# A two-layer decoder trunk on one core: the token factor of the input RMSNorm is applied to the projections' results instead of to their operand

## The chip, the cores and the metric

One Trainium2 chip, one of its cores. The kernel is a single program on that core; its time is the device time of one execution in microseconds (us). The median of three executions before the change is 2590.63 us (2590.49 to 2591.32).

## The reference, cut to what matters

Two identical layers run over 256 tokens with 2048 channels, in float32. Of one layer, what the change touches is this:

```python
h = rmsnorm(x, pre_norm)            # x * rsqrt(mean(x*x) + eps) * pre_norm
proj = h @ w_in                     # 2048 x 21728 combined input projection
(m_z, m_xbc, m_dt, f_q, f_k, f_v, f_f, f_gate, g_q, g_k, g_v, g_lr, g_gate,
 l_cq, l_ckv, l_kr, l_gate, merge) = jnp.split(proj, ...)
xbc = jax.nn.silu(causal_depthwise_conv(m_xbc, conv_w, conv_b))   # a convolution over tokens
...                                  # four branches: SSD, forgetting attention, GLA, latent attention
gates = jax.nn.sigmoid(merge.reshape(bsz, s, N_BRANCHES, D_MODEL))
mixed = sum(gates[:, :, b] * (out[b] @ w_branch[b]) for b in range(4))
return x + rmsnorm(mixed @ w_out, post_norm)
```

The norm has two factors: one per channel (`pre_norm`) and one per token (the reciprocal root of that token's mean square). A factor per token commutes with the projection: `(r * x * pre) @ w = r * ((x * pre) @ w)`.

## The kernel before, in words

All large products are made in float32 precision out of three float32r matmuls: each operand is split into a rounded part and a remainder (`hh` and `hl` for the normed and transposed x, `hi` and `lo` for a weight tile), and hi·hh, lo·hh and hi·hl are accumulated. Weights come as 512 KB tiles `raw` of 128x1024, through the SyncE DMA queue into five buffers; `fetch` (L154) lets ScalarE copy a tile to `hi` (L158) and VectorE subtract to get `lo` (L159). `hi` and `lo` have three buffers each, so the split runs up to two tiles ahead of TensorE.

`chunk_a` (L165) makes 512 output columns for both 128-token blocks (tt = 0 and 1) in one two-bank accumulator `acc`: 16 slices k of the 2048 channels, by two token blocks, by three matmuls of 128x512 are 96 matmuls. Its result has tokens on the partitions. `chunk_b` (L186) makes the transposed result, 4 blocks of 128 output channels on the partitions by 256 tokens, with 192 matmuls of 128x256. There are two `acc` buffers, so a result has to be read out before the next chunk but one begins. The very first chunk of a layer (`acc_c`, L368) takes its first three weight tiles as one group: k = 0 to 5 for token block 0, then k = 0 to 5 for block 1, and from k = 6 on both blocks in turn.

The input norm is `norm_x` (L307). For one token block it sums the squares of x on ScalarE (L238), gets the factor r by a power on GpSimd (L62), multiplies x by r on VectorE (L316 in the first layer; L318 in the second, where the row `prow` with the channel factor is multiplied in as well), transposes the product on TensorE in four tiles of four 128x128 blocks (L321, `tr_x`, two PSUM buffers), and splits the transposed tile into `hh` on ScalarE (L325, L330) and `hl` on VectorE (L327, L331). In the first layer the channel factor comes in there, as a per-partition scalar `vec`. The second layer's x is the end of the first: with the last output projection `acc_y` in hand, L862 adds the post-normed rows to the residual `xr`, in four pieces of 512 columns for each token block, and `norm_x` starts from there.

The order within each engine is set by a scheduler that places the program's instructions by a simulated timeline; work of a background generator (`bg`, `step`, `drain`) is written between the weight tiles of a chunk. Each engine then runs its own list strictly in order and waits on semaphores. The attention, GLA and SSD cores run in such generators beside the projections.

Of the kernel before, what the change touches and what calls it, by code (L numbers as in the profile page):

```python
# [37 lines left out]
def trunk(ctx: ExitStack, tc: tile.TileContext, x, pos, vecs, rows, dskip, pre, post, glaw2,  # L38
# [33 lines left out]
    nc.scalar.dma_start(ident, consts[:, C_ID:C_ID + P])  # L72
    vec = cp.tile([P, DEPTH, V_N], F32, tag="vec", name="vec")
    nc.scalar.dma_start(vec, vecs.rearrange("l p v -> p l v"))
# [16 lines left out]
    def mask_tables():  # L91
        cst = sl.tile([P, 2048], F32, tag="s7", name="cst")
        nc.sync.dma_start(cst[:, :C_N], consts)
        nc.sync.dma_start(caus, consts[:, C_CAUS:C_CAUS + P])
        nc.sync.dma_start(negm, consts[:, C_NEGM:C_NEGM + P])
        S.copy(id2, cst[:, C_ID2:C_ID2 + 32])
        V.tensor_copy(lvl, cst[:, C_LVL:C_LVL + 1024].rearrange("p (a b) -> p a b", a=8))
        yield
# [55 lines left out]
    def fetch(src, n=1024, own=None):  # L154
        raw = st.tile([P, 1024], F32, tag="raw", name="raw", bufs=5)
        nc.sync.dma_start(raw[:, :n], src)
        hi, lo = own or (st.tile([P, 1024], F32R, tag=t, name=t, bufs=3) for t in ("hi", "lo"))
        S.copy(hi[:, :n], raw[:, :n])  # L158
        V.tensor_tensor(lo[:, :n], raw[:, :n], hi[:, :n].bitcast(F32), ALU.subtract)  # L159
        return hi, lo  # L160
# [146 lines left out]
    def norm_x(tt, src, dst, ssq, prow):  # L307

        tot = small([P, 1], f"xtot{tt}")
        V.tensor_reduce(tot, ssq, AX.X, ALU.add)  # L310
        r = rstd(tot, D, 1, f"xn{tt}")
        ts_ = slice(tt * P, (tt + 1) * P)
        for c in range(4):
            cs = slice(c * 512, (c + 1) * 512)
            if prow is None:
                V.tensor_scalar(dst[:, cs], src[:, cs], r, None, ALU.mult)  # L316
            else:
                V.scalar_tensor_tensor(dst[:, cs], src[:, cs], r, prow[:, cs], ALU.mult, ALU.mult)  # L318
            pt = psT(f"tr_x{tt}{c}").rearrange("p (b t) -> p b t", b=4)
            for j in range(4):  # L320
                PE.transpose(pt[:, j], dst[:, c * 512 + j * P:c * 512 + (j + 1) * P], ident)  # L321
            if prow is None:
                pw = lambda j: vec[:, 0, V_PRE + 4 * c + j:V_PRE + 4 * c + j + 1]
                for j in range(4):
                    S.activation(hh[:, 4 * c + j, ts_], pt[:, j], AF.Copy, scale=pw(j))  # L325
                for j in range(4):
                    V.scalar_tensor_tensor(hl[:, 4 * c + j, ts_], pt[:, j], pw(j),  # L327
                                           hh[:, 4 * c + j, ts_].bitcast(F32), ALU.mult, ALU.subtract)
            else:
                S.copy(hh[:, 4 * c:4 * c + 4, ts_], pt)  # L330
                V.tensor_tensor(hl[:, 4 * c:4 * c + 4, ts_], pt, hh[:, 4 * c:4 * c + 4, ts_].bitcast(F32),  # L331
                                ALU.subtract)
# [7 lines left out]
    ssq0 = small([P, 2, 2], "xssq")  # L340
    junk0 = slot(6, "junk")
    for tt in range(2):
        for c in range(2):
            cs = slice(c * 1024, (c + 1) * 1024)
            sumsq(xt[tt][:, cs], junk0[:, cs], ssq0[:, tt, c:c + 1])
        norm_x(tt, xt[tt], slot(2 + tt, "xn"), ssq0[:, tt], None)

    for l in range(DEPTH):
# [15 lines left out]
        for i in range(2):  # L364
            if l == 0 and i == 1:
                bg.append(mask_tables())
                bg.append(rope_tables())
            acc = chunk_a(w_in[l], nxt(8), 16, hh, hl, 0, "acc_c", [3, 1, 1, 1, 1, 1] if i == 0 else None)  # L368
            S.copy(cc[:, i], acc)
            for tt in range(2):  # L370
                sumsq(acc[:, tt], ropej[:, 0:2].rearrange("p a t -> p (a t)"), cssq[:, 2 * i + tt:2 * i + tt + 1])
# [12 lines left out]
        raw2 = slot(6, "raw2")  # L384
        krope, krr = raw2[:, 1024:1024 + T], raw2[:, 1280:1280 + T]
# [130 lines left out]
        for i in range(2):  # L516
            acc = chunk_b(w_in[l], nxt(8), 4, hh, hl, "acc_g")
            if i == 0:
                S.activation(gqk[:, i], acc, AF.Copy, scale=128 ** -0.5)
            else:  # L520
                V.tensor_copy(gqk[:, i], acc)
# [147 lines left out]
        for c in range(3):  # L669
            acc = chunk_b(w_in[l], nxt(8), 4, hh, hl, "acc_x")  # L670
            dst = xsT[:, 4 * c:4 * c + 4] if c < 2 else bcT[:, 0:4]
            for j in range(4):
                b = 4 * c + j
                cw = lambda i: vc(V_CW + 4 * b + i)
                S.activation(dst[:, j], acc[:, j], AF.Identity, bias=vc(V_CB + b), scale=cw(3))
                for i in range(1, 4):
                    V.scalar_tensor_tensor(dst[:, j, i:], acc[:, j, :T - i], cw(3 - i), dst[:, j, i:],
                                           ALU.mult, ALU.add)
# [152 lines left out]
        if not last:  # L831
            prow = load_row(4, pre, l + 1, "prow")
# [7 lines left out]
        ssq = small([P, 2, 4], "xssq4")  # L840
        for c in range(4):
# [9 lines left out]
            for tt in range(2):  # L851
# [8 lines left out]
                for q in range(4):  # L860
                    qs = slice(q * 512, (q + 1) * 512)
                    V.scalar_tensor_tensor(xr[tt][:, qs], yt[tt][:, qs], r, xr[tt][:, qs], ALU.mult, ALU.add)  # L862
                    if not last:
                        sumsq(xr[tt][:, qs], yt[tt][:, qs], ssq[:, tt, q:q + 1])
# [5 lines left out]
                if not last:  # L870
                    norm_x(tt, xr[tt], yt[tt], ssq[:, tt], prow)
# [21 lines left out]
def _layout(inp):  # L893
# [37 lines left out]
    for lv in range(7):  # L931
# [8 lines left out]
            "dskip": inp["d_skip"], "pre": inp["pre_norm"], "post": inp["post_norm"], "glaw2": inp["gla_w2"], "w_sm": w_sm, "w_in": w_in,  # L940
# [20 lines left out]
```

## Time and profile before

| what | value |
|---|---|
| median of 3 executions | 2590.63 us |
| the profiled execution: its own time / the span of its instructions | 2591.68 us / 2589.3 us |
| VectorE busy in the span | 1531.6 us (59%) |
| ScalarE busy in the span | 1248.9 us (48%) |
| DMA moved / mean rate | 461.48 MB / 178 GB/s |
| mean granted TensorE clock | 0.997 |

A row of the timeline view gives the start in us from the span's start, the duration in us, the engine, the source line, the operation with output and inputs, how many equal instructions were merged, and in brackets how long the engine had been idle and what released it. ACT is ScalarE, DVE is VectorE, POOL is GpSimd, SPq and ACTq are the DMA-issuing queues of SyncE and ScalarE. Matmul durations overlap, so the distance between two starts is what a matmul costs TensorE. In the waits view a row reads "engine, tile, line, released by": total us, times, longest.

### The profile page before, as it was taken

What the parts mean: (1) busy time and instruction counts of PE and PEld (TensorE: products, weight loads), DVE (VectorE), ACT (ScalarE), POOL (GpSimd) and SP (SyncE); (2) the same over time, 40 slices, a digit from 0 to 9 for tenths busy, and PEclk for the clock granted to TensorE, in tenths of its full rate; (3) what the DMA queues carried; (4) which work ended last, traced back from release to release, by engine and by line L of the source; (5) the groups of instructions that cost most, each with busy time, mean ns of one, the idle gap of its engine ahead of it and who ended that gap; (6) DMA issues with size and microseconds to landing.
All of it is one profiled execution on the core that took longest, in us unless ns stands there. A gap on an engine that the chain in (4) does not pass through costs nothing.

```text
span 2589.3 us, 34775 instructions
## 1 busy us (share of the span) xinstructions
PE 2558.0 (99%) x13810; PEld 2208.8 (85%) x13810; DVE 1531.6 (59%) x1886; ACT 1248.9 (48%) x1589; POOL 25.1 (1%) x33
## 2 busy tenths in 40 slices
PE   8999999999999999999989999999999999999998
PEld 6898888988899888888878988889888998888887
DVE  6755855676654455555557568546766545555554
ACT  5654544455444445444455445444555444544443
POOL 0000000000000000000000000000000000000000
PEclk9999999999999999999999999999999999999999
DMA  6554555555555555655645445555555555556554
GB/s 228 181 161 147 170 164 186 183 178 170 179 195 180 173 177 173 209 189 182 211 158 186 155 147 175 168 180 185 174 173 189 185 177 176 169 166 206 191 179 155
DMA packets 126722, 461.48 MB, mean 178 GB/s; under 512 B 14656, under 2 KB 15168, under 8 KB 125664
## 3 DMA queue, kind: packets, MB, share of 16 engines
q1 hardware_dynamic: 126144, 459.11, 54.7%
q8 instruction: 108, 1.77, 0.3%
q14 instruction: 54, 0.44, 0.0%
q10 hardware_dynamic: 416, 0.17, 0.0%
HBM read 455.02 MB, written 4.19 MB: 177 GB/s over the span
## 4 chain that ended last, share of the span: by engine, by line
PE 98%; ACT 1%; DVE 1%; issue 0%; DMA 0%; POOL 0%; SPq 0%; DVEq 0%; POOLq 0%; ACTq 0%
PE acc_f L196 2%; PE acc_f L195 2%; PE acc_f L194 2%; PE acc_mC L180 2%; PE acc_mD L180 2%; PE acc_mA L180 2%; PE acc_mC L179 2%; PE acc_mA L179 2%; PE acc_mD L179 2%; PE acc_mA L181 2%; PE acc_mC L181 2%; PE acc_mD L181 2%; PE acc_mB L181 2%; PE acc_mB L180 2%; PE acc_mB L179 2%; PE acc_y L181 2%
## 5 line engine op out<-in xcount | busy, mean ns | idle before, releaser
L159 DVE TENSOR_TENSOR lo<-raw,hi 128x1024 fp32r<-128x1024 f32 x842 | 1027.4, 1222 | 851.0 <-ACT hi L158 848.0
L158 ACT CAST hi<-raw 128x1024 fp32r<-128x1024 f32 x842 | 882.0, 1049 | 1106.8 <-PE acc_f L195 109.8
L196 PE MATMUL acc_f<-hh,lo 128*128 128x256 f32 x512 | 145.1, 283 | 0.0
L195 PE MATMUL acc_f<-hl,hi 128*128 128x256 f32 x512 | 145.0, 283 | 0.0
L194 PE MATMUL acc_f<-hh,hi 128*128 128x256 f32 x512 | 144.9, 283 | 0.0
L196 PE MATMUL acc_x<-hh,lo 128*128 128x256 f32 x384 | 108.9, 284 | 0.0
L195 PE MATMUL acc_x<-hl,hi 128*128 128x256 f32 x384 | 108.7, 283 | 0.0
L194 PE MATMUL acc_x<-hh,hi 128*128 128x256 f32 x384 | 108.7, 283 | 0.0
L180 PE MATMUL acc_mC<-lo,hh 128*128 128x512 f32 x256 | 104.6, 409 | 0.0
L180 PE MATMUL acc_mD<-lo,hh 128*128 128x512 f32 x256 | 103.1, 403 | 0.0
L180 PE MATMUL acc_mA<-lo,hh 128*128 128x512 f32 x256 | 102.7, 401 | 0.0
L179 PE MATMUL acc_mA<-hi,hh 128*128 128x512 f32 x256 | 101.9, 398 | 0.0
L179 PE MATMUL acc_mC<-hi,hh 128*128 128x512 f32 x256 | 100.5, 393 | 0.0
L180 PE MATMUL acc_mB<-lo,hh 128*128 128x512 f32 x256 | 100.2, 392 | 0.0
L181 PE MATMUL acc_mA<-hi,hl 128*128 128x512 f32 x256 | 100.1, 391 | 0.0
L179 PE MATMUL acc_mD<-hi,hh 128*128 128x512 f32 x256 | 100.0, 391 | 0.0
L181 PE MATMUL acc_mD<-hi,hl 128*128 128x512 f32 x256 | 99.8, 390 | 0.0
L181 PE MATMUL acc_mC<-hi,hl 128*128 128x512 f32 x256 | 99.8, 390 | 0.0
L181 PE MATMUL acc_mB<-hi,hl 128*128 128x512 f32 x256 | 99.7, 389 | 0.0
L179 PE MATMUL acc_mB<-hi,hh 128*128 128x512 f32 x256 | 99.7, 389 | 0.0
L194 PEld LDWEIGHTS acc_f<-hh,hi 128*128 128x128 f32 x512 | 98.3, 192 | 0.1
L195 PEld LDWEIGHTS acc_f<-hl,hi 128*128 128x128 f32 x512 | 98.3, 192 | 0.1
(419 smaller groups left out, 6040.6 us busy)
## 6 DMA issues: line engine op xcount, KB each, us to landing
raw<-in_w_in_dram SPq DMA_DIRECT2D x624, 512.0 KB, 3.4
raw<-in_w_br_dram SPq DMA_DIRECT2D x128, 512.0 KB, 3.4
raw<-in_w_out_dram SPq DMA_DIRECT2D x64, 512.0 KB, 3.4
raw<-in_w_ukv_dram SPq DMA_DIRECT2D x16, 512.0 KB, 4.3
raw<-in_w_uq_dram SPq DMA_DIRECT2D x12, 512.0 KB, 3.3
x<-in_x_dram SPq DMA_DIRECT2D x4, 512.0 KB, 5.8
xr<-in_x_dram SPq DMA_DIRECT2D x2, 1024.0 KB, 6.1
pn<-in_post_dram SPq DMA_DIRECT2D x2, 1024.0 KB, 7.0
```

The lines of the kernel that those rows point to most:

```text
L158: S.copy(hi[:, :n], raw[:, :n])
L159: V.tensor_tensor(lo[:, :n], raw[:, :n], hi[:, :n].bitcast(F32), ALU.subtract)
L179: PE.matmul(a2[tt], xh[:, k0 + k, ts_], hi[:, c], start=(k == 0), stop=False)
L180: PE.matmul(a2[tt], xh[:, k0 + k, ts_], lo[:, c], start=False, stop=False)
L181: PE.matmul(a2[tt], xl[:, k0 + k, ts_], hi[:, c], start=False, stop=(k == nk - 1))
L194: PE.matmul(acc[:, b], hi[:, c], xh[:, k], start=(k == 0), stop=False)
L195: PE.matmul(acc[:, b], hi[:, c], xl[:, k], start=False, stop=False)
L196: PE.matmul(acc[:, b], lo[:, c], xh[:, k], start=False, stop=(k == 15))
```

## The change

x goes to the transposes as it is, and the transposed tile is multiplied by the channel factor while it is split, in both layers now (`feed`). The token factor is worked out beside that (`factor`, a background generator), with one power for both token blocks, and is kept in two forms: `rt`, tokens on the partitions, and `rb`, tokens along the free axis and the same on all partitions, which two small matmuls with the identity make. Every reading of a projection's result multiplies by one of the two: per-partition scale on ScalarE (`scale_out`, the sigmoids), `scalar_tensor_tensor` with `rt` on VectorE, or a product with `rb` for the transposed results. In the first layer the DMAs are issued in another order as well: `vec` before `ident` on ScalarE's queue; on SyncE's queue the first three weight tiles between and behind the pieces of x, and the small tables `rc`, `row`, `dsk` behind the tile `cst`.

```diff
+    vec = cp.tile([P, DEPTH, V_N], F32, tag="vec", name="vec")
+    nc.scalar.dma_start(vec, vecs.rearrange("l p v -> p l v"))
+    ident = cp.tile([P, P], F32, tag="ident", name="ident")
+    nc.scalar.dma_start(ident, consts[:, C_ID:C_ID + P])
+    first_raw = []
     for tt in range(2):
         for c in range(2):
             cs = slice(c * 1024, (c + 1) * 1024)
             nc.sync.dma_start(xt[tt][:, cs], x[tt * P:(tt + 1) * P, cs])
-    ident = cp.tile([P, P], F32, tag="ident", name="ident")
-    nc.scalar.dma_start(ident, consts[:, C_ID:C_ID + P])
-    vec = cp.tile([P, DEPTH, V_N], F32, tag="vec", name="vec")
-    nc.scalar.dma_start(vec, vecs.rearrange("l p v -> p l v"))
+        for i in (0, 1, 2)[2 * tt:2 * tt + 2]:
+            first_raw.append(st.tile([P, 1024], F32, tag="raw", name="raw", bufs=5))
+            nc.sync.dma_start(first_raw[-1], w_in[0][i])
...
-    def silu_gate(acc, dst, name):
-
-        S.activation(dst, acc, AF.Sigmoid)
-        V.tensor_tensor(dst, acc, dst, ALU.mult)
+    def silu_gate(acc, dst):
+
+        for tt in range(2):
+            S.activation(dst[:, tt], acc[:, tt], AF.Sigmoid, scale=rt[:, tt:tt + 1])
+        for tt in range(2):
+            V.scalar_tensor_tensor(dst[:, tt], acc[:, tt], rt[:, tt:tt + 1], dst[:, tt], ALU.mult, ALU.mult)
+
+    def scale_out(acc, dst):
+        for tt in range(2):
+            S.activation(dst[:, tt], acc[:, tt], AF.Copy, scale=rt[:, tt:tt + 1])
...
+    def feed(tt, c, src, l):
+
+        ts_ = slice(tt * P, (tt + 1) * P)
+        pt = psT(f"tr_x{tt}{c}").rearrange("p (b t) -> p b t", b=4)
+        for j in range(4):
+            PE.transpose(pt[:, j], src[:, c * 512 + j * P:c * 512 + (j + 1) * P], ident)
+        pw = lambda j: vec[:, l, V_PRE + 4 * c + j:V_PRE + 4 * c + j + 1]
+        for j in range(4):
+            S.activation(hh[:, 4 * c + j, ts_], pt[:, j], AF.Copy, scale=pw(j))
+        for j in range(4):
+            V.scalar_tensor_tensor(hl[:, 4 * c + j, ts_], pt[:, j], pw(j),
+                                   hh[:, 4 * c + j, ts_].bitcast(F32), ALU.mult, ALU.subtract)
+
+    def factor(src, junk):
+
+        ssq = small([P, 2, 2], "xssq")
+        for tt in range(2):
+            for c in range(2):
+                cs = slice(c * 1024, (c + 1) * 1024)
+                sumsq(src[tt][:, cs], junk[tt][:, cs], ssq[:, tt, c:c + 1])
+                yield
+        tot = small([P, 2], "xtot")
         V.tensor_reduce(tot, ssq, AX.X, ALU.add)
...
+        r = rstd(tot, D, 2, "xn")
+        V.tensor_copy(rt, r)
+        yield
+        pt = psT("rbp")[:, :T]
+        for tt in range(2):
+            PE.matmul(pt[:, tt * P:(tt + 1) * P], rt[:, tt:tt + 1].to_broadcast([P, P]), ident, start=True, stop=True)
+        V.tensor_copy(rb, pt)
+        yield
...
-            S.copy(cc[:, i], acc)
+            if i == 0:
+                drain()
+            scale_out(acc, cc[:, i])
...
             acc = chunk_b(w_in[l], nxt(8), 4, hh, hl, "acc_x")
             dst = xsT[:, 4 * c:4 * c + 4] if c < 2 else bcT[:, 0:4]
+            gt = st.tile([P, 4, T], F32, tag="gt", name="gt")
+            V.tensor_tensor(gt, acc, rb3(ALLP, 4), ALU.mult)
+            acc = gt
...
                 if i == 1:
-                    S.copy(fk0[0:64, cs], acc[0:64])
-                    V.tensor_copy(fk1[64:128, cs], acc[64:128])
-                elif c == 0:
-                    S.copy(fq[:, cs], acc)
+                    V.tensor_tensor(fk0[0:64, cs], acc[0:64], rb3(slice(0, 64), 4), ALU.mult)
+                    V.tensor_tensor(fk1[64:128, cs], acc[64:128], rb3(slice(64, P), 4), ALU.mult)
                 else:
-                    V.tensor_copy(fq[:, cs], acc)
+                    V.tensor_tensor(fq[:, cs], acc, rb3(ALLP, 4), ALU.mult)
...
-        if not last:
-            prow = load_row(4, pre, l + 1, "prow")
...
                     if not last:
-                        sumsq(xr[tt][:, qs], yt[tt][:, qs], ssq[:, tt, q:q + 1])
+                        feed(tt, q, xr[tt], l + 1)
...
-                if not last:
-                    norm_x(tt, xr[tt], yt[tt], ssq[:, tt], prow)
+        if not last:
+            bg.append(factor(xr, yt))
```

The scheduler gives the engines new lists. Three places matter here. The first is ScalarE at the very start of the program. `junk,xssq<-x` is the sum of squares of half a token block, `hh<-tr_x` four blocks of the split, `hi<-raw` a weight tile; the number behind `tr_x` counts tiles. Before:

```order
L238 ACTIVATE junk,xssq<-x_0_70 128x1024 x2
L238 ACTIVATE junk,xssq<-x_1_71 128x1024 x2
L399 ACTIVATE mult<-row 32x1 x2
L325 ACTIVATE hh<-tr_x_112,vec 128x128 x4
L325 ACTIVATE hh<-tr_x_126,vec 128x128 x4
L158 CAST hi<-raw 128x1024 x3
L325 ACTIVATE hh<-tr_x_140,vec 128x128 x4
```

After, at the same place:

```order
L245 ACTIVATE junk,xssq<-x_0_70 128x1024 x2
L336 ACTIVATE hh<-tr_x_105,vec 128x128 x4
L165 CAST hi<-raw 128x1024
L336 ACTIVATE hh<-tr_x_118,vec 128x128 x4
L165 CAST hi<-raw 128x1024
L245 ACTIVATE junk,xssq<-x_1_71 128x1024
L336 ACTIVATE hh<-tr_x_131,vec 128x128 x4
L245 ACTIVATE junk,xssq<-x_1_71 128x1024
L165 CAST hi<-raw 128x1024
L336 ACTIVATE hh<-tr_x_144,vec 128x128 x4
L336 ACTIVATE hh<-tr_x_157,vec 128x128 x4
```

The split of the first tile moved ahead of the sums of the second token block and of the tables; the weight tiles are spread between.

The second place is VectorE between the layers, from the end of the first layer's last projection on (`ytot` and `yn_ms` belong to the post norm, `gs` to a small weight of the next layer). Before:

```order
L862 SCALAR_TENSOR_TENSOR xr_9870<-y_9868,yn_rs,xr_9870 128x512 x4
L855 TENSOR_REDUCE ytot_10533<-yssq 128x1
L857 TENSOR_TENSOR y_9869<-acc_y_10336,pn 128x512
L60 TENSOR_SCALAR yn_ms<-ytot_10533 128x1
L310 TENSOR_REDUCE xtot_10494<-xssq_9882 128x1
L862 SCALAR_TENSOR_TENSOR xr_9871<-y_9869,yn_rs,xr_9871 128x512
L60 TENSOR_SCALAR xn_ms<-xtot_10494 128x1
L862 SCALAR_TENSOR_TENSOR xr_9871<-y_9869,yn_rs,xr_9871 128x512 x3
L448 TENSOR_TENSOR gs<-raw_10951,gs 16x512 x2
L318 SCALAR_TENSOR_TENSOR y_9868<-xr_9870,xn_rs,prow 128x512 x4
L310 TENSOR_REDUCE xtot_10550<-xssq_9882 128x1
L331 TENSOR_TENSOR hl<-tr_x_10501,hh 128x4x128
```

After:

```order
L885 SCALAR_TENSOR_TENSOR xr_9904<-y_9902,yn_rs,xr_9904 128x512 x4
L878 TENSOR_REDUCE ytot_10574<-yssq 128x1
L880 TENSOR_TENSOR y_9903<-acc_y_10367,pn 128x512
L60 TENSOR_SCALAR yn_ms<-ytot_10574 128x1
L338 SCALAR_TENSOR_TENSOR hl<-tr_x_10516,vec,hh 128x128 x4
L885 SCALAR_TENSOR_TENSOR xr_9905<-y_9903,yn_rs,xr_9905 128x512 x4
L338 SCALAR_TENSOR_TENSOR hl<-tr_x_10530,vec,hh 128x128 x4
L476 TENSOR_TENSOR gs<-raw_11020,gs 16x512 x2
L338 SCALAR_TENSOR_TENSOR hl<-tr_x_10545,vec,hh 128x128 x4
L350 TENSOR_REDUCE xtot<-xssq 128x2
L338 SCALAR_TENSOR_TENSOR hl<-tr_x_10559,vec,hh 128x128 x4
L60 TENSOR_SCALAR xn_ms<-xtot 128x2
```

The multiplications by the factor (L318) are gone, the first `hl` stands ahead of the second token block's residual, and the second `hl` stands behind it.

The third place is VectorE in the convolution of the SSD branch, at the end of a chunk `acc_x` (`lo` is the split of the next weight tiles). Before:

```order
L159 TENSOR_TENSOR lo<-raw,hi 128x1024 x6
L677 SCALAR_TENSOR_TENSOR xsT<-acc_x,vec,xsT 128x255
L677 SCALAR_TENSOR_TENSOR xsT<-acc_x,vec,xsT 128x254
L677 SCALAR_TENSOR_TENSOR xsT<-acc_x,vec,xsT 128x253
L159 TENSOR_TENSOR lo<-raw,hi 128x1024
L677 SCALAR_TENSOR_TENSOR xsT<-acc_x,vec,xsT 128x255
```

After:

```order
L699 TENSOR_TENSOR gt<-acc_x,rb 128x1024
L166 TENSOR_TENSOR lo<-raw,hi 128x1024
L706 SCALAR_TENSOR_TENSOR xsT<-gt,vec,xsT 128x255 x2
L706 SCALAR_TENSOR_TENSOR xsT<-gt,vec,xsT 128x254
L706 SCALAR_TENSOR_TENSOR xsT<-gt,vec,xsT 128x255
L706 SCALAR_TENSOR_TENSOR xsT<-gt,vec,xsT 128x254
L706 SCALAR_TENSOR_TENSOR xsT<-gt,vec,xsT 128x255
L706 SCALAR_TENSOR_TENSOR xsT<-gt,vec,xsT 128x253
L706 SCALAR_TENSOR_TENSOR xsT<-gt,vec,xsT 128x254
L166 TENSOR_TENSOR lo<-raw,hi 128x1024
```

A multiplication came in front, and where three convolution steps stood between two `lo`, eight stand now.

More of the change, by code (lines that the diff above doesn't have):

```diff
@@ L37, in trunk @@
 @with_exitstack
-def trunk(ctx: ExitStack, tc: tile.TileContext, x, pos, vecs, rows, dskip, pre, post, glaw2,
+def trunk(ctx: ExitStack, tc: tile.TileContext, x, pos, vecs, rows, dskip, post, glaw2,
           w_sm, w_in, w_uq, w_ukv, w_br, w_out, consts, ropec, out):
@@ L93, in mask_tables @@
         nc.sync.dma_start(cst[:, :C_N], consts)
+        nc.sync.dma_start(rc, ropec)
+        nc.sync.dma_start(row, rows.rearrange("l p v -> p l v"))
+        nc.sync.dma_start(dsk, dskip.rearrange("(o l) h -> o l h", o=1).to_broadcast([P, DEPTH, 16]))
         nc.sync.dma_start(caus, consts[:, C_CAUS:C_CAUS + P])
@@ L154, in fetch @@
     def fetch(src, n=1024, own=None):
-        raw = st.tile([P, 1024], F32, tag="raw", name="raw", bufs=5)
-        nc.sync.dma_start(raw[:, :n], src)
+        if first_raw:
+            raw = first_raw.pop(0)
+        else:
+            raw = st.tile([P, 1024], F32, tag="raw", name="raw", bufs=5)
+            nc.sync.dma_start(raw[:, :n], src)
         hi, lo = own or (st.tile([P, 1024], F32R, tag=t, name=t, bufs=3) for t in ("hi", "lo"))
@@ L238, in sumsq, with rb3 @@
         S.activation(junk, src, AF.Square, accum_out=acc)
-    def silu_gate(acc, dst, name):
-        S.activation(dst, acc, AF.Sigmoid)
-        V.tensor_tensor(dst, acc, dst, ALU.mult)
+    rt = cp.tile([P, 2], F32, tag="rt", name="rt")
+    rb = cp.tile([P, T], F32, tag="rb", name="rb")
+    def rb3(p_, n):
+        return rb[p_].rearrange("p (o t) -> p o t", o=1).to_broadcast([p_.stop - p_.start, n, T])
+    ALLP = slice(0, P)
+    def silu_gate(acc, dst):
[6 more added lines that the diff above has]
+            S.activation(dst[:, tt], acc[:, tt], AF.Copy, scale=rt[:, tt:tt + 1])
     def attention(npair, dv, scale, terms, bias, v, gate, name):
@@ L304, in attention @@
             yield
-    def norm_x(tt, src, dst, ssq, prow):
-        tot = small([P, 1], f"xtot{tt}")
-        V.tensor_reduce(tot, ssq, AX.X, ALU.add)
[L311 to L332, printed above, removed]
@@ L339, in trunk @@
     xs_dram = [None]
-    ssq0 = small([P, 2, 2], "xssq")
-    junk0 = slot(6, "junk")
     for tt in range(2):
[L343 to L346, printed above, removed]
+        for c in range(4):
+            feed(tt, c, xt[tt], 0)
+    bg.append(factor(xt, [slot(2 + tt, "junk") for tt in range(2)]))
     for l in range(DEPTH):
@@ L384, in trunk @@
         raw2 = slot(6, "raw2")
+        acc = accs
+        accs = raw2[:112, 1536:1536 + T]
+        V.tensor_tensor(accs, acc[:112], rb[:112], ALU.mult)
         krope, krr = raw2[:, 1024:1024 + T], raw2[:, 1280:1280 + T]
@@ L517, in trunk @@
             acc = chunk_b(w_in[l], nxt(8), 4, hh, hl, "acc_g")
[L518 to L521, printed above, removed]
+            V.scalar_tensor_tensor(gqk[:, i], acc, 1.0 if i else 128 ** -0.5, rb3(ALLP, 4), ALU.mult, ALU.mult)
         gv = slot(6, "gv").rearrange("p (a b) -> p a b", a=2)
@@ L538, in merge @@
                 gt = st.tile([P, 2, 512], F32, tag="gt", name="gt")
-                S.activation(gt, acc, AF.Sigmoid)
+                for tt in range(2):
+                    S.activation(gt[:, tt], acc[:, tt], AF.Sigmoid, scale=rt[:, tt:tt + 1])
                 bi = "ABCD".index(br)
@@ L678, in trunk @@
                                            ALU.mult, ALU.add)
-            gt = st.tile([P, 4, T], F32, tag="gt", name="gt")
             S.activation(gt, dst, AF.Sigmoid)
@@ L785, in trunk @@
             acc = chunk_a(w_in[l], nxt(8), 16, hh, hl, 0, "acc_fv")
-            S.copy(fv[:, :, c * 512:(c + 1) * 512], acc)
+            scale_out(acc, fv[:, :, c * 512:(c + 1) * 512])
         drain(sg)
@@ L839, in trunk @@
         dst = out if last else xs_dram[0]
-        ssq = small([P, 2, 4], "xssq4")
         for c in range(4):
@@ L939, in _layout @@
     return {"x": inp["x"].reshape(T, D), "pos": inp["positions"].reshape(1, T), "vecs": vecs, "rows": rows,
-            "dskip": inp["d_skip"], "pre": inp["pre_norm"], "post": inp["post_norm"], "glaw2": inp["gla_w2"], "w_sm": w_sm, "w_in": w_in,
+            "dskip": inp["d_skip"], "post": inp["post_norm"], "glaw2": inp["gla_w2"], "w_sm": w_sm, "w_in": w_in,
             "w_uq": w_uq, "w_ukv": w_ukv, "w_br": w_br, "w_out": w_out, "consts": c, "ropec": rc}
```

15 lines of the change are left out of this document (6 added, 9 removed).

## The prediction

> **What bounds the kernel now.** I read the page's busy shares first, then TensorE's waits, then the timeline around each wait.
>
> ```profile
> PE 2558.0 (99%) x13810; PEld 2208.8 (85%) x13810; DVE 1531.6 (59%) x1886; ACT 1248.9 (48%) x1589; POOL 25.1 (1%) x33
> PE tr_x L321 <- DVE xn L316: 9.0, 1, 9.0
> PE tr_x L321 <- DVE y L318: 7.6, 1, 7.6
> PE acc_c L179 <- ACT hi L158: 2.7, 1, 2.7
> PE tr_m L220 <- DVE m_l L224: 1.5, 2, 0.7
> ```
>
> TensorE is busy for 2558.0 of 2589.3 us. Its two long waits are for the two norms: 9.0 us until the first normed x, and 7.6 us between the layers. Everything between loses under 4 us. So the change can gain only in two stretches, at the start and between the layers, and can lose wherever it makes TensorE wait in the 2500 us that have no wait now. I take as a mark in each stretch the read-out of the first `acc_c`, which starts when its 96 matmuls are done.
>
> **The start.**
>
> ```profile
> 4.67 1.06 ACT L238 ACTIVATE junk<-x 128x1024 f32<-128x1024 f32 x1 [1.74 <-DMA x<-in_x_dram]
> 9.01 1.97 PE L321 MATMUL tr_x<-ident,xn 128*128 128x128 f32 x8 [9.01 <-DVE xn L316]
> 10.62 2.09 ACT L325 ACTIVATE hh<-tr_x,vec 128x128 fp32r<-128x128 f32 x8
> 12.62 2.92 ACT L158 CAST hi<-raw 128x1024 fp32r<-128x1024 f32 x3
> 15.24 3.48 DVE L159 TENSOR_TENSOR lo<-raw,hi 128x1024 fp32r<-128x1024 f32 x3
> 16.50 0.80 PE L180 MATMUL acc_c<-lo,hh 128*128 128x512 f32 x1
> 18.80 0.63 PE L179 MATMUL acc_c<-hi,hh 128*128 128x512 f32 x1
> 19.23 0.63 PE L180 MATMUL acc_c<-lo,hh 128*128 128x512 f32 x1
> 20.26 0.40 PE L180 MATMUL acc_c<-lo,hh 128*128 128x512 f32 x1
> 20.50 0.39 PE L181 MATMUL acc_c<-hi,hl 128*128 128x512 f32 x1
> 43.51 1.01 ACT L369 COPY cc<-acc_c 128x1024 f32<-128x1024 f32 x1 [1.31 <-PE acc_c L181]
> 0.72 0.41 ACTq L72 DMA_DIRECT2D ident<-in_consts_dram  x1
> 1.16 0.45 ACTq L74 DMA_DIRECT2D vec<-in_vecs_dram  x1
> vec<-in_vecs_dram ACTq DMA_DIRECT2D x1, 98.0 KB, 6.7
> ident<-in_consts_dram ACTq DMA_DIRECT2D x1, 64.0 KB, 4.1
> ```
>
> The dense stream of matmuls begins at 16.50, at a pitch of 0.43 us (18.80 to 19.23) until about 20, and of 0.23 us after that; the mark is 43.5.
>
> What goes: the wait of the transposes for sums, power and product. What is late next: `ident`. It landed 4.1 us after its issue at 0.72, that is at 4.8, and `vec`, second on that queue, at 1.16 + 6.7 = 7.9. The two are swapped, so `ident` lands between 4.8 and 7.9; I take 7.9, since it is now the second of the same two. The transposes of the first tile (half of 1.97) then end at 8.9.
>
> From there ScalarE's list sets the pace: four blocks of `hh` take 2.09/2 = 1.05 us, a `hi` 2.92/3 = 0.97, a sum 1.06. In the new order hh, hi, hh, hi, sum, hh, sum, hi, hh, hh from 8.9 on, the last of these (the first `hh` of token block 1) ends at 19.3. VectorE follows about 1.2 us behind a `hi` (3.48/3 for a `lo`): first `lo` at 12.3, third at 18.8. Up to there TensorE has done little: 13 of the 36 matmuls of k = 0 to 5, at the slow pitch and between waits. From 18.8 it has 23 matmuls and two transposed tiles (about 0.55 us each at the fast pitch) before k = 6: 23 x 0.23 + 1.1 = 6.4 us, and up to 1.5 us more while the pitch is slow; then 60 matmuls x 0.227 = 13.6, one more tile 0.55 and the two small matmuls for `rb`, 0.3. The mark comes at 39.7 to 41.2; I take 40.4, **3.1 us earlier**. The bounds: 38.5 (5 us) if `ident` lands early, 41.9 (1.6 us) if the pitch stays slow or a `lo` is late. The tables moved behind `cst` land no later than ScalarE needs them: `cst` itself held ScalarE by 0.8 us before, until 18.45, and it now stands behind the `hh` that ends at 19.3.
>
> ```profile
> 18.45 0.22 ACT L96 CAST id<-cst 128x32 fp32r<-128x32 f32 x1 [0.79 <-DMA cst<-in_consts_dram]
> ```
>
> **Between the layers.**
>
> ```profile
> 1291.75 2.74 DVE L862 SCALAR_TENSOR_TENSOR xr<-y,yn_rs,xr 128x512 f32<-128x512 f32 x4 [0.67 <-POOL yn_rs L62]
> 1293.20 0.39 PE L181 MATMUL acc_y<-w_last,m_l 128*128 128x512 f32 x1
> 1293.83 0.58 ACT L238 ACTIVATE gt<-acc_y 128x512 f32<-128x512 f32 x1
> 1295.42 0.56 POOL L62 TENSOR_TENSOR yn_rs<-yn_ms,neghalf 128x1 f32<-128x1 f32 x1 [3.70 <-DVE yn_ms L60]
> 1298.84 1.38 DVE L448 TENSOR_TENSOR gs<-raw,gs 16x512 fp32r<-16x512 f32 x2
> 1300.26 2.74 DVE L318 SCALAR_TENSOR_TENSOR y<-xr,xn_rs,prow 128x512 f32<-128x512 f32 x4
> 1301.15 1.94 PE L321 MATMUL tr_x<-ident,y 128*128 128x128 f32 x8 [7.56 <-DVE y L318]
> 1308.48 0.60 PE L321 MATMUL tr_x<-ident,y 128*128 128x128 f32 x4
> 1315.84 6.22 SPq L156 DMA_DIRECT2D raw<-in_w_in_dram  x4
> 1330.28 1.01 ACT L369 COPY cc<-acc_c 128x1024 f32<-128x1024 f32 x1 [1.67 <-PE acc_c L181]
> ```
>
> The first two pieces of `xr` are ready at 1293.1, before TensorE ends `acc_y` at 1293.6. Before, the transposes still waited for sums, power and L318 until 1301.15. Now they follow at once and end at 1294.7 (8 x 0.13, from the 0.60 for four). What is late next is worked out along the lists. ScalarE: a sum of 1024 columns from 1293.2 (1.06, and its read-out), then the square of `acc_y` 0.58, so the first `hh` come at 1295.0 to 1296.1, the next to 1297.1. VectorE: the second token block's post norm ends about 0.5 us later than before, at 1296.6; first `hl` at 1297.1; `xr` of block 1 (2.74) to 1299.8; second `hl` (1.1) 1300.9; `gs` (1.38) 1302.3; third `hl` 1303.4; two more tiles to 1305.9.
>
> TensorE: k = 0 to 3 go with the first `hl`, to 1299; k = 4 then waits for the second `hl` until 1300.1; k = 5 ends at 1301.1. The next transposes need a `tr_x` buffer, of which there are two, and the one they get is free only after the third `hl`: a wait of about 1.8 us to 1303.4. Block 1 then starts at 1304.5, waits once for its `hl` to 1305.5, and runs dense: 16 matmuls and a tile to 1309.7, 60 more, a tile and `rb` to 1324.1. Against 1330.1 that is 6.0 us. On SyncE's queue the stores of `xr` now wait for the later second block, up to 1299.8, with weight tiles queued behind them; that costs nothing, since the five buffers are full by then and the next tile was issued only at 1315.84. The load of `prow` that goes hid beside the last projection, and gives nothing.
>
> The clock takes part of it back.
>
> ```profile
> 1296.00:1298.00 2.00, 0.00 (x0) 0.00 (x0) 1.99 (x4) 1.79 (x4) 0.99 (x1) 0.64 0.41 168
> 1306.00:1308.00 2.00, 2.00 (x8) 1.60 (x7) 1.73 (x3) 0.00 (x0) 0.00 (x0) 0.80 0.00 0
> 2580.00:2585.00 5.00, 1.07 (x5) 0.56 (x3) 4.33 (x10) 0.69 (x2) 0.56 (x1) 0.84 0.51 210
> ```
>
> The number ahead of the last two is the granted clock. It fell to half at 1296.6 (0.64 over two us), 3 us after the last matmul, and came back at 1306.8, 5.7 us after the transposes had begun again. At the end of the program a mean of 0.84 over five us puts the fall at 2583.4, only 2.3 us after the last matmul (2580 + 1.07), though 1.07 us of matmuls lie in the 3.4 us before it. In my schedule TensorE does 0.9 us of matmuls from 1299.6 to 1304.5, less than that share. So I expect the clock to fall there and to stay down for 2 to 5.7 us of dense work, each costing half of itself: 1 to 2.9 us, I take 2.0. **4.0 us earlier**, with bounds of 2 and 6.
>
> The Trainium skill, page "TensorE: Matmul & The Clock Gate", in its part on the HAM clock gate, says that the clock is halved after an idle window of about 3.4 us. By that rule no gap of this schedule (the longest is 1.8 us) halves it, and the whole 6.0 us would be kept. The row of the program's end, where 1.07 us of work did not keep the clock up, speaks for a window that need not be wholly idle.
>
> **The rest of both layers.** The read-outs cost more on two engines that have room.
>
> ```profile
> L159 DVE TENSOR_TENSOR lo<-raw,hi 128x1024 fp32r<-128x1024 f32 x842 | 1027.4, 1222 | 851.0 <-ACT hi L158 848.0
> L158 ACT CAST hi<-raw 128x1024 fp32r<-128x1024 f32 x842 | 882.0, 1049 | 1106.8 <-PE acc_f L195 109.8
> 488.92 1.23 DVE L159 TENSOR_TENSOR lo<-raw,hi 128x1024 fp32r<-128x1024 f32 x1 [1.65 <-ACT hi L158]
> 490.06 1.51 DVE L677 SCALAR_TENSOR_TENSOR xsT<-acc_x,vec,xsT 128x255 f32<-128x255 f32 x3
> 491.80 1.23 DVE L159 TENSOR_TENSOR lo<-raw,hi 128x1024 fp32r<-128x1024 f32 x1 [0.23 <-ACT hi L158]
> L675 ACT ACTIVATE xsT<-acc_x,vec x16: 559/560/563, 488.8 to 1808.0; 128x256 f32<-128x256 f32 x16
> ```
>
> VectorE gets, in each layer, some six products of 1024 columns (1.22 us each, as `lo`) that are new or were ScalarE's: three for the convolution, one of gqk, two of fq and fk; and a third of one for the small projections, and 0.1 to 0.2 us for each of eight gates cut in two. That is some 9 us a layer. It hides in the 851 us that VectorE idles ahead of `lo`; ScalarE's few extra starts and two more table loads hide in its 1107 us. If that cover were gone, 18 us would show.
>
> The one place with little cover is the convolution. A weight tile lasts 2.88 us there (488.92 to 491.80). `hi`, then `lo`, are made when a buffer comes free, two tiles (5.8 us) ahead of use; they take 2.3, so `lo` may come about 3.4 us late. After a chunk's end VectorE now does the product (1.2), a `lo` (1.2), eight steps (8 x 0.50 = 4.0) and the next `lo` (1.2): 7.7 us, where TensorE reaches that tile after 3 x 2.88 = 8.6. Slack 0.9 us. I take 0.5 us lost over the six chunks and the other read-outs; below, nothing (a buffer that comes free earlier can't shorten a stream without waits), above, what the whole convolution ahead of one `lo` costs: 1.2 + 12 x 0.50 - 3.4 = 3.8 us a chunk, 23 us.
>
> The sum: 3.1 + 4.0 - 0.5 = 6.6 us off the profiled execution's 2591.68, so 2585.1. The median before is 1.05 below that execution, so I say **2584.0**.
>
> **Rivals.**
> - *The clock holds.* If TensorE's share of work between the layers is enough, 6.0 stays, and with 3.6 at the start the gain is 9 to 10: 2581. For it: only short gaps. Against: the end-of-program row.
> - *The waits move.* The norm's wait goes, but `ident`, the third `hl` behind `xr` and `gs`, and a slow clock take its place, so that the lower bounds hold: 1.6 + 2 - 0.5 = 3 us, 2587.5, within 0.2%. For it: VectorE's list between the layers, where a `tr_x` buffer waits behind 4.1 us of other work. Against: each of those rows is short.
> - *VectorE becomes the bound in the convolution.* From about 2 us lost in each of the six chunks the gain is gone and 5 us more: 2596; at 3.8 us each, 2607. It decides once the eight steps start more than 0.9 us later than I reckon, for instance because each waits for its ScalarE step of 0.56 us. Against: these run ahead during the `lo` in between.
> - *The factor is waited for after all.* The first read-out of `acc_c` needs `rt`. Its last sum is early (about 16.6 at the start, 1303 between the layers), the read-outs 20 us later; then nothing is lost. I give it almost nothing.
>
> **How the numbers follow.** A measurement of this kernel can tell about 0.2%, 5.2 us, from no change. Forecast (5.2 to 8 us gained) 0.45; the clock holds 0.20; the waits move 0.28; slower by over 5.2 us 0.07. Faster is the first two, 0.65; the same 0.28; slower 0.07. The range goes from both upper bounds, 5 + 6 = 11 us (2579.5), to 1.6 us gained, 2589; it leaves out the convolution's case and a little of the third.
>
> **What would show it.** TensorE's waits for L316 and L318 must be gone; the first matmul of the second layer must come at about 1.7 us after `acc_y`; the mark must come about 30.5 us after the end of `acc_y` (36.5 before) with the transposes for block 1 waiting for VectorE; the mark at the start at about 40.4; no wait for `lo` in `acc_x`. I am wrong if TensorE's busy time rises by more than 2 us, if new waits of over 2 us stand between 45 and 1285 us, or if the first transposes start after 9.

## The result, and the profile after

The change made the kernel slower by 11.6 us, 0.4%: a median of 2602.23 us (2600.83 to 2602.78) against 2590.63 before, ratio 1.0043 with a 95% interval of 1.003 to 1.0057. The forecast was 2584.0. The profiled execution took 2601.53 us, its span 2599.7.

From the page of the changed kernel, the busy times, and from the view of its waits, TensorE's longest (us in total, times, longest):

```profile
PE 2575.6 (99%) x13818; PEld 2200.4 (85%) x13818; DVE 1541.3 (59%) x1926; ACT 1263.4 (49%) x1659; POOL 23.8 (1%) x31
PE tr_x L333 <- DMA ident<-in_consts_dram: 7.3, 1, 7.3
PE tr_x L333 <- DVE xtot L350: 1.7, 1, 1.7
PE tr_m L227 <- DVE m_l L231: 1.5, 2, 0.7
PE acc_c L186 <- ACT hi L165: 1.3, 1, 1.3
```

The two long waits for the norm are gone. At the start the wait for `ident` (7.3 us) stands where that for the norm was (9.0), and no other wait is over 2 us. Yet TensorE is busy for 17.6 us more (2575.6 against 2558.0). The eight additional matmul records out of 13818 are those that make `rb`, 1.2 us of it. Nothing waits longer; the same matmuls take longer.

The timeline of the changed kernel at the marks (start, duration, engine, line, what it makes):

```profile
7.29 1.94 PE L333 MATMUL tr_x<-ident,x 128*128 128x128 f32 x8 [7.29 <-DMA ident<-in_consts_dram]
39.24 1.27 ACT L264 ACTIVATE cc<-acc_c,rt 128x512 f32<-128x512 f32 x2 [1.75 <-PE acc_c L188]
1299.22 0.39 PE L188 MATMUL acc_y<-w_last,m_l 128*128 128x512 f32 x1
1299.45 1.03 PE L333 MATMUL tr_x<-ident,xr 128*128 128x128 f32 x8
1301.25 0.50 PE L186 MATMUL acc_c<-hi,hh 128*128 128x512 f32 x1 [0.76 <-ACT hh L336]
1309.43 0.66 PE L333 MATMUL tr_x<-ident,xr 128*128 128x128 f32 x4 [1.70 <-DVE xtot L350]
1331.04 1.27 ACT L264 ACTIVATE cc<-acc_c,rt 128x512 f32<-128x512 f32 x2 [1.75 <-PE acc_c L188]
```

The first read-out of `acc_c` comes at 39.24 (43.51 before), `acc_y` ends at 1299.22 + 0.39 = 1299.61 (1293.59), the second layer's read-out comes at 1331.04 (1330.28). The differences between these marks split the span; the last column belongs to the first experiment.

| part of the span, us | before | changed | rt and rb last |
|---|---|---|---|
| start to the first read-out | 43.51 | 39.24 (-4.3) | 38.21 (-5.3) |
| from there to the end of `acc_y` | 1250.08 | 1260.37 (+10.3) | 1249.93 (-0.2) |
| to the second layer's read-out | 36.69 | 31.43 (-5.3) | 32.45 (-4.2) |
| to the end | 1259.03 | 1268.63 (+9.6) | 1258.17 (-0.9) |

Both stretches gained more than forecast, and the two middles lost 19.9 us. In a matmul's row the operand named first is the one that is streamed (128x512 or 128x256), and the second is the one that is loaded ahead of it as weights (128*128). Windows of TensorE alone over two chunks that hold nothing else, of before and of the changed kernel (window, length, busy and count, granted clock, DMA share, GB/s): first a chunk `acc_mB` of 96 matmuls with `hh` or `hl` loaded, from its first start to that of the next chunk, then `acc_bB`, 48 matmuls of the same shape with `oB_h` or `oB_l` loaded. (The counts include matmuls that reach over an edge.)

```profile
1136.50:1158.26 21.76, 21.76 (x98) 1.00 0.61 194
1158.26:1169.14 10.88, 10.88 (x50) 1.00 0.62 193
```

```profile
1141.24:1163.64 22.40, 22.40 (x98) 1.00 0.61 189
1163.64:1174.53 10.89, 10.89 (x50) 1.00 0.59 188
```

At a full clock, without a gap, `acc_mB` takes 22.40/96 = 0.2333 us a matmul instead of 0.2267; `acc_bB` stays at 0.2267. Over the first layer the mean start-to-start times by projection give +13.0 us for the 128x512 matmuls with `hh` or `hl` loaded and -2.2 us for the 128x256 ones that stream them, 10.8 in all (a part of it lies ahead of the first mark): the whole of the +10.3 us.

What do the slow ones share? The tiles' places as the program was built, in bytes along a partition:

```
             before   changed  rt,rb last  rt 64 bytes  before+32  rt,rb ahead
hh           25344    25344    25344       25344        25344      26400
rt           -        58112    228032      58112        -          25344
hi (first)   94976    96032    94976       96064        95008      96032
hi - hh      69632    70688    69632       70720        69664      69632
  mod 256    0        32       0           64           32         0
```

All six buffers of `hi` and `lo` lie a multiple of 4096 from each other, and `hl` lies 16384 behind `hh`, so they share the remainder. `rt`, 8 bytes in a slot of 32, and `rb`, 1024 bytes, stand behind `hl` in the pool `cp`, and move what lies behind by 1056. `oB_h`, in the same pool as `hi`, moves along with it.

### The profile page after: what moved, and what is told of

Read it like the earlier page. It is cut to its first block, busy times and chain, and to the rows that moved or that the text cites. A ratio compares the mean times of both kernels' runs of the same rounds, so it can differ in the third digit from the quotient of the medians.

```text
span 2599.7 us, 34902 instructions
## 1 busy us (share of the span) xinstructions
PE 2575.6 (99%) x13818; PEld 2200.4 (85%) x13818; DVE 1541.3 (59%) x1926; ACT 1263.4 (49%) x1659; POOL 23.8 (1%) x31
## 4 chain that ended last, share of the span: by engine, by line
PE 98%; ACT 1%; DVE 1%; issue 0%; DMA 0%; POOL 0%; DVEq 0%; POOLq 0%; ACTq 0%
PE acc_mC L187 2%; PE acc_f L203 2%; PE acc_f L201 2%; PE acc_f L202 2%; PE acc_mA L187 2%; PE acc_mD L187 2%; PE acc_mA L186 2%; PE acc_mB L187 2%; PE acc_mC L188 2%; PE acc_mC L186 2%; PE acc_mB L186 2%; PE acc_mB L188 2%; PE acc_mA L188 2%; PE acc_mD L188 2%; PE acc_mD L186 2%; PE acc_y L188 2%
```

## Experiments

Theory A (place): the pace hangs on the distance between what is loaded and what is streamed. Theory B (work): the additional read-out passes slow TensorE. Theory C (data): operands that are not normed do.

### The changed kernel with rt and rb last

```diff
+    rp = ctx.enter_context(tc.tile_pool(name="rp", bufs=1))   # behind sm
-    rt = cp.tile([P, 2], F32, tag="rt", name="rt")
-    rb = cp.tile([P, T], F32, tag="rb", name="rb")
+    rt = rp.tile([P, 2], F32, tag="rt", name="rt")
+    rb = rp.tile([P, T], F32, tag="rb", name="rb")
```

> The changed kernel with rt and rb in a pool opened behind all others, so that every tile behind hh and hl lies as far from them as before the change (hi 69632 bytes behind hh, where the changed kernel has 70688); nothing else differs. Theory A (place): a 128x512 matmul that has hh or hl loaded goes at 0.234 instead of 0.227 us because hi and lo now lie 32 bytes off the 64-byte grid of hh and hl. It expects 0.227 us here, 0.120 for acc_f again (0.117 in the changed kernel), the 1250 us between the two first read-outs of acc_c and the layer's end within 1.5 us of before, and 2580 to 2585 us in all (start 4.3 to 5 and boundary 5.3 to 6 us earlier than before, 0.5 a layer lost). Theory B (work): the read-outs' additional passes on VectorE and ScalarE hold up TensorE's operands. It expects no change from the changed kernel: 2602, 0.234 us. Theory C (data): operands that are not normed make matmuls slower. Also 2602, 0.234 us.

2580.59 us, ratio 0.9959 (0.9945 to 0.9974). The marks in the timeline of this run:

```profile
6.62 1.94 PE L334 MATMUL tr_x<-ident,x 128*128 128x128 f32 x8 [6.62 <-DMA ident<-in_consts_dram]
7.74 1.14 ACT L337 ACTIVATE hh<-tr_x,vec 128x128 fp32r<-128x128 f32 x4 [0.33 <-PE tr_x L334]
38.21 1.27 ACT L265 ACTIVATE cc<-acc_c,rt 128x512 f32<-128x512 f32 x2 [1.67 <-PE acc_c L189]
1287.75 0.39 PE L189 MATMUL acc_y<-w_last,m_l 128*128 128x512 f32 x1
1320.59 1.27 ACT L265 ACTIVATE cc<-acc_c,rt 128x512 f32<-128x512 f32 x2 [1.67 <-PE acc_c L189]
```

They give the last column of the table above. The two chunks, in windows of this run:

```profile
1131.05:1152.81 21.76, 21.76 (x98) 1.00 0.63 195
1152.81:1163.69 10.88, 10.88 (x50) 1.00 0.60 197
```

The same work and the same data at 0.2267 us, with the instructions of every compute engine in the same order as in the changed kernel: B and C fall. With only the two tiles moved, the change gains 10.8 us over before (2591.41 in these rounds).

### The kernel before with 32 bytes more

```diff
+    pad = cp.tile([P, 8], F32, tag="pad", name="pad")   # behind hl
+    V.memset(pad, 0.0)
```

> The kernel before with one tile of 32 bytes behind hl, written once and never read: operands, read-outs and order are those of before, and hi and lo lie 32 bytes further from hh. Theory A expects the whole loss: 0.234 us for 128x512 with hh or hl loaded, 0.117 for acc_f, acc_b and acc_y at 0.227 as before, and 20 us more, 2609 to 2613. Theories B and C expect 2590.6 and 0.227 us.

2612.51 us, ratio 1.0081 (1.0066 to 1.0096), 21 us lost by a tile that nobody reads, in the same two chunks:

```profile
1146.00:1168.39 22.39, 22.39 (x97) 1.00 0.59 189
1168.39:1179.28 10.89, 10.89 (x49) 1.00 0.59 191
```

### rt and rb ahead of hh

```diff
+    rt = cp.tile([P, 2], F32, tag="rt", name="rt")
+    rb = cp.tile([P, T], F32, tag="rb", name="rb")
     hh = cp.tile([P, 16, T], F32R, tag="hh", name="hh")
     hl = cp.tile([P, 16, T], F32R, tag="hl", name="hl")
...
-    rt = cp.tile([P, 2], F32, tag="rt", name="rt")
-    rb = cp.tile([P, T], F32, tag="rb", name="rb")
```

> The changed kernel with rt and rb ahead of hh in their pool instead of behind hl: hi and lo keep their addresses (96032, 32 bytes off the 64-byte grid), and hh and hl move with them, so that hi lies 69632 bytes behind hh as before the change. If the distance between what is loaded and what is streamed counts, 128x512 goes at 0.227 us again and the time is that of rt and rb behind all others, 2579 to 2583. If the place of hi and lo alone counts (their own grid), nothing is gained over the changed kernel: 0.234 us, 2602; and then acc_c to acc_z stay slow while acc_b and acc_y do not.

2580.87 us, ratio 0.996 (0.9946 to 0.9974), although `hi` and `lo` stand where they stand in the changed kernel:

```profile
1131.50:1153.26 21.76, 21.76 (x98) 1.00 0.62 193
1153.26:1164.14 10.88, 10.88 (x50) 1.00 0.61 197
```

So it is the distance that counts, not the place of either.

### rt in 64 bytes

```diff
-    rt = cp.tile([P, 2], F32, tag="rt", name="rt")
+    rt = cp.tile([P, 16], F32, tag="rt", name="rt")[:, 0:2]
```

> The changed kernel with rt's tile 64 bytes long in place of 8 (which take a slot of 32), so that hi and lo lie 1088 bytes further behind hh than before instead of 1056. Theory A with a grid of 64 bytes expects the same as with rt and rb behind all others: 0.227 us, 2580 to 2585. Theory A with a grid of 128 bytes or more expects some other pitch than 0.227. Theories B and C expect 2602 and 0.234 us.

2568.31 us, ratio 0.9911 (0.9895 to 0.9928): 12 us better than any theory said, so my grid of 64 bytes fell. At distance 64 `acc_mB` takes a little more than at 0 (21.98/96 = 0.2290 us), and the matmuls that stream `hh` take much less:

```profile
1124.96:1146.94 21.98, 21.98 (x97) 1.00 0.60 193
749.83 0.28 PE L202 MATMUL acc_f<-hl,hi 128*128 128x256 f32 x1
749.94 0.28 PE L203 MATMUL acc_f<-hh,lo 128*128 128x256 f32 x1
750.05 0.28 PE L201 MATMUL acc_f<-hh,hi 128*128 128x256 f32 x1
750.16 0.28 PE L202 MATMUL acc_f<-hl,hi 128*128 128x256 f32 x1
```

Three steps of `acc_f` take 0.33 to 0.34 us here. Before, in the same place:

```profile
749.82 0.28 PE L194 MATMUL acc_f<-hh,hi 128*128 128x256 f32 x1
749.94 0.28 PE L195 MATMUL acc_f<-hl,hi 128*128 128x256 f32 x1
750.05 0.28 PE L196 MATMUL acc_f<-hh,lo 128*128 128x256 f32 x1
750.18 0.28 PE L194 MATMUL acc_f<-hh,hi 128*128 128x256 f32 x1
```

There they take 0.36.

### The distance, swept

`hi` and `lo` get 128 spare columns, and each projection uses them from another byte:

```diff
+    OFFS = {"acc_lg": (16, 16), "acc_gv": (32, 32), ...}    # bytes for hi and lo, by projection
...
-        hi, lo = own or (st.tile([P, 1024], F32R, tag=t, name=t, bufs=3) for t in ("hi", "lo"))
+        hi, lo = own or (st.tile([P, 1152], F32R, tag=t, name=t, bufs=3)[:, o // 4:o // 4 + 1024]
+                         for t, o in zip(("hi", "lo"), off[0]))
```

> The changed kernel with rt and rb last, raw in four buffers instead of five, and hi and lo in tiles of 1152 columns, used from another byte in each projection: lg 16, gv 32, gg 48, z 64, fv 8, fg 4, mC 96, mD 128, mA hi alone 32, mB lo alone 32, bA 32, bC 64, bD 16, acc_g 16, the acc_x chunks 32, 64 and 48, the acc_f chunks 0, 8, 96 and 128; the others 0. Theory A with a grid of 64 bytes expects 0.234 us at 32 and 96 and 0.227 at 0, 64 and 128 for 128x512, the reverse kind of step (0.117 against 0.120) for the chunks that stream hh, and 0.234 in bA too, though there oA is loaded instead of hh; what 4, 8, 16 and 48 do is open. With mA and mB it tells whether hi or lo matters each for itself. Theories B and C expect one pitch for all offsets. The total time says nothing here.

A second run took the distances left open:

> As the first kernel with an offset for each projection, with other bytes: lg 192, gv 256, gg 320, z 384, fv 448, fg 504, mA 256, mB 448, mC 192, acc_g 72, acc_x chunks 56, 64 and 192, acc_f chunks 256, 320, 384 and 448; the others 0. A grid of 256 bytes expects 0.227 us at 256 as at 0; a grid of 512 or more expects another pitch there. Which offsets are fast for 128x256 is open; 64 should give 0.113 or 0.118 again. The total time says nothing.

The two took 2600.58 and 2587.55 us, one execution each; only their matmuls are compared.

From the records of these two runs and of the one with rt and rb last: the start of a matmul to the start of the next, in ns, against the distance from what is streamed to the weights loaded meanwhile (336 to 7358 records a column, without the intervals that hold a wait; the distances are those of `hi` and `lo` behind `hh` and `hl`, in bytes; the matmuls of `acc_mA` and `acc_mB` in the first run, where only one of the two was moved, stand each at its own distance, 0 or 32):

```
128x512, hh loaded:    0    4    8   16   32   48   64   96  128  192  256  320  384  448  504
  median             227  237  235  231  233  232  229  232  232  233  227  229  231  233  232
128x256, hh streamed:  0    8   16   32   48   56   64   72   96  128  192  256  320  384  448
  median             120  115  118  117  119  118  117  118  117  119  117  120  118  119  118
```

0 and 256 read alike, and so within 1 ns do 64 and 320, 128 and 384, 192 and 448: as far as these go, what counts is the remainder by 256. The 128x512 are fastest at 0 and 256, and there the 128x256 are slowest. The 117 of the 128x256 at 64 is a median over two paces, 113 and 118. `acc_bA`, at distance 32 from `oA_h` in the first run, went at 234 ns instead of 227, so this is not peculiar to `hh`. In `acc_mA` and `acc_mB`, shifting `hi` alone or `lo` alone slowed all three kinds of matmul (means 230 to 233 ns).

### A distance for each kind

```diff
+        off[0] = 16      # chunk_b alone, in elements; 0 elsewhere
```

> rt and rb last; hi and lo in tiles of 1152 columns (raw in four buffers to make room), used from their start where hh is loaded (128x512) and from byte 64 where hh is streamed (128x256: acc_g, acc_x, acc_f). If each kind of matmul has its own best distance and nothing else hangs on it, the 128x512 keep the 0.227 to 0.236 us of distance 0 and the 3456 of 128x256 go at 0.1135 to 0.118 instead of 0.120 us: 7 to 22 us less than 2580.6, so 2558 to 2574. If the gain of the 64-byte run came from the rest of the layout (slots, raw, oh all moved as well), it is 2580 as with rt and rb last.

2569.12 us, ratio 0.9914 (0.9899 to 0.9929). The 128x512 were back at 227.6 ns in `acc_mB`, but `acc_f` had a mean of 117.3 ns, where it had 114.8 in the 64-byte run. At distance 64 a chunk runs at 113 or at 118 ns for dozens of matmuls on end, much alike in both layers, and here most of `acc_f` ran at 118. Which of the two it falls into is not settled. The next run keeps the 64-byte layout, and moves `hi` and `lo` back to a multiple of 256 for `chunk_a` only:

```diff
-    rt = cp.tile([P, 2], F32, tag="rt", name="rt")
+    rt = cp.tile([P, 16], F32, tag="rt", name="rt")[:, 0:2]
...
+        off[0] = 112 if xh is hh else 0     # chunk_a: 448 bytes
+        off[0] = 0                          # chunk_b
+        off[0] = 16                         # chunk_b4: 64 bytes
```

> The run with rt in 64 bytes (everything behind hl 64 bytes off hh's grid of 512), and hi and lo in tiles of 1152 columns, used from byte 448 where hh is loaded (so 512 behind hh's grid), from 0 where hh is streamed (distance 64), and from 64 where oh is streamed; raw in four buffers. If pace hangs on the distance for each kind of matmul, 128x512 goes as with distance 0 (some 1.3 us in a thousand matmuls less than in the 64-byte run, 7 us in all) and 128x256 at 0.1135 us for the most part as there: 2558 to 2563. If the 128x256 fall to 0.118 as in the run with two distances, 2566 to 2569.

2562.06 us, ratio 0.9888 (0.9871 to 0.9904): the fastest of all runs, 40 us below the changed kernel, with as many instructions at other addresses and one `raw` buffer less (at the start, a few on ScalarE and VectorE stand in another order). `acc_f` stayed at 114.8 ns, `acc_mB` went at 227.9, `acc_uq` at 117.8 instead of 119.9.

### The parts of the start

The kernel before, with the new order of loads alone:

```diff
+        for i in (0, 1, 2)[2 * tt:2 * tt + 2]:
+            first_raw.append(st.tile([P, 1024], F32, tag="raw", name="raw", bufs=5))
+            nc.sync.dma_start(first_raw[-1], w_in[0][i])
...
-    nc.sync.dma_start(rc, ropec)      # and row, dsk: now behind cst; vec's load now ahead of ident's
```

> The kernel before with nothing but the changed kernel's order of loads at the start: vec ahead of ident, the first weight tiles between the pieces of x, the small tables behind cst; the norm stays ahead of the transposes. If the start's gain (5.3 us with rt and rb last) is the norm's wait that went, the first read-out of acc_c comes within 0.7 us of 43.5 and the time is 2590 to 2591.5. If the order of the loads makes part of the gain, it comes by that part earlier: 2 us would be 41.5 and 2588.6.

2588.31 us, ratio 0.999 (0.998 to 0.9999). The first matmul of `acc_c` in the timeline of the kernel before, then that matmul and the mark in this run:

```profile
13.70 0.79 PE L179 MATMUL acc_c<-hi,hh 128*128 128x512 f32 x1 [2.73 <-ACT hi L158]
```

```profile
10.59 0.78 PE L186 MATMUL acc_c<-hi,hh 128*128 128x512 f32 x1
40.98 1.01 ACT L376 COPY cc<-acc_c 128x1024 f32<-128x1024 f32 x1
```

So the order of loads by itself moves the mark 2.5 us, with the norm's wait still there: the wait for the first `hi` goes, and the matmuls reach the pitch of 0.23 us at about 13 instead of 20 us. Which part each of the two has, the runs do not show. That the norm's leaving is worth the remaining 2.8 of the 5.3 us is a difference, not a measurement of its own: the engines' lists changed as well. Then `ident` ahead of `vec`, on the version with rt and rb last:

```diff
+    ident = cp.tile([P, P], F32, tag="ident", name="ident")
+    nc.scalar.dma_start(ident, consts[:, C_ID:C_ID + P])
     vec = cp.tile([P, DEPTH, V_N], F32, tag="vec", name="vec")
```

> rt and rb last, and ident's load ahead of vec's on ScalarE's queue, as before the change. If ident holds the start, the transposes begin at about 5 instead of 6.6 us, and the first read-out of acc_c, at 38.2 with rt and rb last, comes up to 1.5 us earlier: 2579. If vec, now second and needed by the first hh, holds it in ident's place, the read-out comes within 0.5 us of 38.2: 2580.6.

2579.36 us, ratio 0.9956 (0.9941 to 0.9971), and its timeline:

```profile
4.82 1.97 PE L334 MATMUL tr_x<-ident,x 128*128 128x128 f32 x8 [4.82 <-DMA ident<-in_consts_dram]
7.35 2.18 ACT L337 ACTIVATE hh<-tr_x,vec 128x128 fp32r<-128x128 f32 x8
38.37 1.27 ACT L265 ACTIVATE cc<-acc_c,rt 128x512 f32<-128x512 f32 x2 [1.67 <-PE acc_c L189]
```

The transposes start 1.8 us earlier, but the first `hh` only 0.4 (7.74 with rt and rb last), and the mark stays (38.37 against 38.21): `ident` does not hold the start alone. The scheduler also made other lists for the start, and TensorE waits there for an `hl`, as the waits of this run show:

```profile
PE tr_x L334 <- DVE hl L339: 2.9, 1, 2.9
```

The 1.2 us in the total are about what the clock cost in the profiled pair, below.

## Why the prediction was wrong

**The step that failed** is "The rest of both layers". It priced the read-outs on VectorE and ScalarE and took TensorE's stream for fixed: its lower bound was "nothing", since a stream without waits cannot shorten, and its upper one was a late `lo`. Every matmul was carried over from before at 0.227 us. The sum had no term for the pace of the matmuls, and none of the rivals did. Two lines of the diff, `rt = cp.tile` and `rb = cp.tile` between `hl` and all that follows, set that pace for 5760 matmuls: +0.5 us was forecast, +19.9 came (with the 3456 of 128x256, which gained a little). With the two tiles elsewhere the same term measures -1.0 (-0.2 and -0.9): the read-outs do hide, and TensorE waits for no `lo` in `acc_x`. One of the signs named beforehand as proof of an error, TensorE's busy time up by more than 2 us, is what appeared, without the other, a new wait.

**The start**: -3.1 forecast, -4.3 measured, inside the bounds of 1.6 and 5, and -5.3 with rt and rb last, a little past them. Of the 1.0 us between these two runs not all is the distance: in the second, `ident` landed 0.67 us earlier (6.62 against 7.29; 7.9 was forecast). The mechanism was right and its size too small; the new order of loads, worth 2.5 us by itself, was not priced as a term.

**Between the layers**: -4.0 forecast, -5.3 measured. The order came as worked out: first matmul 1.64 us after `acc_y` (1.7 forecast), a wait of 1.70 us for VectorE ahead of block 1's transposes (1.8), the mark 31.43 us after the end of `acc_y` (30.5 before the clock's part). The clock did not fall in this execution, so the 2.0 us taken off for it were not due; that is luck, since in the run with rt and rb last, with the same lists, it did (below). Some 0.6 us of the mark's delay are the slower pitch (96 matmuls at 0.0066 us).

**The rivals.** "The clock holds" describes what came between the layers, but its 2581 is near the time of the run with rt and rb last, in which the clock fell, and not of the change. The convolution's rival covers the measured time, 2596 to 2607, for a cause that is not there. Slower by over 5.2 us had been given a chance of 0.07. The factor was waited for nowhere.

## What to carry to other kernels

A new tile, here one of 8 bytes, moves the tiles allocated behind it: put small ones last, and after an edit compare the distance (here its remainder by 256) between loaded and streamed operands. When TensorE's busy time changes and its waits do not, take the start-to-start time of one shape, chunk by chunk, before looking for contention. And try other distances on purpose: here that gave 18.5 us (2580.6 to 2562.1) on top of the 10.8 that the change itself gains.

## What the runs showed of the hardware

**The distance between loaded and streamed operands.** 32 bytes cost 128x512 matmuls 3% (0.2267 to 0.2333 us), and 64 bytes gave 128x256 ones up to 6% (0.120 to 0.113). The Trainium skill, page "SBUF — State Buffer", section "Who interferes with whom", gives TensorE two independent read ports, one for the streamed operand and one for loading, and says that it never waits on anyone. The runs show an interplay of the two that the page does not have; what it is inside the chip they do not show.

**The clock between the layers.** In the twelve profiled executions the granted clock changes only at the ends of consecutive windows of 3.413 us, counted from the moment it first rose (in the kernel before, 374.0, 377.0 and 751.0 windows after it). Such windows of TensorE in the changed kernel, and in the run with rt and rb last (window, length, busy and count, clock):

```profile
1304.92:1308.33 3.41, 2.63 (x14) 1.00 0.75 308
1308.33:1311.75 3.42, 1.86 (x11) 1.00 0.00 0
```

```profile
1292.95:1296.36 3.41, 3.10 (x17) 1.00 0.74 304
1296.36:1299.77 3.41, 1.36 (x8) 1.00 0.01 4
1299.77:1303.18 3.41, 3.41 (x12) 0.50 0.00 0
```

And in the run with `ident` first:

```profile
1294.91:1298.33 3.42, 1.72 (x10) 1.00 0.45 186
```

Nearly the same schedule had 1.36 us of work in one window and lost the clock for the next, or 1.86 or 1.72 us and kept it: it depends on where the window's edges fall. Over all these executions, of the windows at full clock those with up to 43% of work halved it, those with 50% or more did not, and 47% did once and did not once; TensorE was busy for 1.36/3.41 = 40% of the one above that did, and for 54% and 50% of the two that did not. From the first `acc_y` to the second layer's `acc_small` it took 145.21 us with the fall and 143.86 with `ident` first: 1.35 us for one window at half clock. The forecast's own reading, that a window need not be wholly idle, holds; the Trainium skill, page "TensorE: Matmul & The Clock Gate", part on the HAM clock gate, has the window's length and that it runs free, but speaks of an idle window.
